# Deferring RMSNorm past the K, V and f projections, with a reordered first stage, in an eight-core attention and gMLP step

## The chip, the cores and the metric

One Trainium2 chip, all eight cores, one launch. Two programs run: even cores (role 0) own 20 of the 32 token blocks of a stream, odd cores (role 1) own the other 12, 32 rows of running streams, and compute K and V of role 0's 20 blocks too, because their attention needs them. The metric is the device time of the slowest core in microseconds. It stands above the spans that the profile lists: by 3.4 to 4.0 us where an even core has the longest span, by 1.0 to 1.1 where an odd one is longest by 3 us or more. Some executions fall into a slower state, in which the cores of one die show a lower granted clock and take longer (in one run of the twelfth kernel 0.816 to 0.830 and 1753 to 1800 us on die 0, against 0.987 to 0.995 and 1520 to 1529 us on die 1); only fast runs are compared.

## The reference, cut to what matters

```python
def rmsnorm(x, g):
    y = x * lax.rsqrt(jnp.mean(x * x, axis=-1, keepdims=True) + RMS_EPS)
    return y * g
def mixer_layer(x, norm_g, w_in, b_f, ln_g, ln_b, w_s, b_s, w_out, caches=None):
    h = rmsnorm(x, norm_g)
    z = h @ w_in                 # columns [q | k | v | f | g_A | u | v_B | g_B], D = 2048
    logf = log_sigmoid(f + b_f)
    v_b  = layernorm(gelu(v_B), ln_g, ln_b)
    out_a = fox_attention(q, k, v, logf) * silu(g_A)      # 8 heads of 128, causal
    out_b = gelu(u) * (tril(w_s) @ v_b + b_s) * silu(g_B) # chunks of 128 positions
    y = x + concat(out_a, out_b) @ w_out                  # a last rmsnorm follows
    return y, k, v, logf, v_b                             # k, v, logf are outputs too
```

With r = 1/sqrt(mean(x²)+eps), one number per token, h @ W = r · ((x·g) @ W). The norm can therefore be applied after a projection as well as before it.

Of the kernel before, what the change touches and what calls it, by code (L numbers as in the profile page):

```python
# [12 lines left out]
D = 2048  # L13
KC = 16
# [106 lines left out]
class Arena:  # L121
# [18 lines left out]
    def alloc(self, name, shape, dt, nres=1, hi=False):  # L140
        n = int(np.prod(shape)) * (4 if dt in (F32, I32) else 2)
        n = (n + 63) // 64 * 64
        gaps = self.gaps(n)
        assert gaps, ("arena full", name, n, [(t.name, t.hi - t.lo) for t in self.live])
        lo = gaps[-1][1] - n if hi else gaps[0][0]
        t = Tile(name, lo, lo + n, shape, dt, self.ap, nres)
        for d in self.dead:
            if d.lo < t.hi and t.lo < d.hi:
                for r in t.res:
                    for o in d.res:  # L150
                        r.inherit(o)
        self.live.append(t)
        self.peak = max(self.peak, max(x.hi for x in self.live))
        return t
# [51 lines left out]
def build_program(only_role=None):  # L206
# [8 lines left out]
    def dscr(name, shape, dt=BF16):  # L215
# [17 lines left out]
        KT_s=dscr("KT_s", [8, 128, NBLK * 128]), V_s=dscr("V_s", [8, 128, NBLK, 129]),  # L233
# [25 lines left out]
def emit(ctx, role):  # L259
# [28 lines left out]
    def load(q, out, in_, res, part=False, reads=()):  # L288
        q.dma(out, in_, dsem_of(res), reads=reads, writes=[] if part else [res], pwrites=[res] if part else [])
# [24 lines left out]
    if smp:  # L314
# [3 lines left out]
    POOL.op(lambda: g.memset(ones[:], 1.0), writes=[ones.r])  # L318
    POOL.op(lambda: g.memset(utri[:], 1.0), writes=[utri.r])
    POOL.op(lambda: g.affine_select(out=utri[:], in_=utri[:], pattern=[[1, 128]], compare_op=ALU.is_ge,  # L320
                                    fill=0.0, base=0, channel_multiplier=-1), reads=[utri.r], writes=[utri.r])
    POOL.op(lambda: g.tensor_scalar(out=utrih[:], in0=utri[:], scalar1=0.5, scalar2=None, op0=ALU.mult), reads=[utri.r], writes=[utrih.r])
# [3 lines left out]
    H = HTok(A, [(t * 512, 512) for t in range(NT)] if role == 0 else [(0, 768), (768, 800)])  # L326
    WK = [A.alloc("WK%d" % h, [KC, 128], BF16) for h in range(8)]
    VW = [384, 384, 264]
    WV = [A.alloc("WV%d" % c, [KC, VW[c]], BF16) for c in range(2 if role == 0 else 3)]
    hTb, Vf, Vb = [], [], []  # L330
    v_ready = False
    xt = [A.alloc("xt%d" % i, [2, KC, 128], F32, nres=2, hi=(i == 2)) for i in range(3)]
    sq = [A.alloc("sq%d" % i, [KC, 64], F32) for i in range(2)]
    ssp = A.alloc("ssp", [256], F32)
    rb = [A.alloc("rb%d" % i, [256], F32) for i in range(2)]
    NKS = 3
    Kb = [A.alloc("Kb%d" % i, [512], BF16) for i in range(NKS)]
    if role:
        Vb = [A.alloc("Vb%d" % i, [8, 129], BF16) for i in range(2)]
    Kf = [A.alloc("Kf%d" % i, [512], F32, hi=True) for i in range(NKS)]  # L340
    R_KTs, R_Vs = Res("KT_s"), Res("V_s")

    xq = []
    if role == 0:
        groups = [("own", list(range(4 * i, 4 * i + 4))) for i in range(NT)]
        passes = [("K", i) for i in range(NT)] + [("V", i) for i in range(NT)]
    else:
        groups = [("own", list(range(4 * i, 4 * i + 4))) for i in range(NT)] + [("smp", [0])]
        groups += [("oth", list(range(4 * i, 4 * i + 4))) for i in range(o0 // 4)]
        passes = [("K", i) for i in range(NT + 1)] + [("V", i) for i in range(NT + 1)]  # L350
        for i in range(NT + 1, len(groups)):
            passes += [("K", i), ("V", i)]
        passes[-3:-1] = [passes[-2], passes[-3]]
    def ng_of(n):
        return 0 if n < 2 else 8

    nunits, pairs = [], []
    for gi, (kind, bl) in enumerate(groups):
        for p0 in range(0, len(bl), 2):
            pr = dict(kind=kind, bl=bl[p0:p0 + 2], tile=None)  # L360
            nunits.append(dict(gi=gi, pr=pr, ii=[p0 + i for i in range(len(pr["bl"]))], kind=kind, bl=pr["bl"]))
            pairs.append(pr)
    xfree = {"tiles": [0, 1, 2], "next": 0}

    def x_next():
        while xfree["next"] < len(pairs):
            pr = pairs[xfree["next"]]
            ok = [t for t in xfree["tiles"] if t < 2 or pr["kind"] != "oth"]
            if not ok:
                return  # L370
            t = pr["tile"] = ok[0]
            xfree["tiles"].remove(t)
            xfree["next"] += 1
            for a, j in enumerate(pr["bl"]):
                if pr["kind"] == "smp":
                    load(SP, xt[t][:, a, :, 0:NS2], io["xsT"], xt[t].res[a])
                else:
                    load(SP, xt[t][:, a, :, :], io["xT"][(o0 if pr["kind"] == "own" else 0) + j], xt[t].res[a])

    def ninfo(n):  # L380
        u = nunits[n]
        rows = NS2 if u["kind"] == "smp" else 128
        na = len(u["ii"])
        t = xt[u["pr"]["tile"]]
        return u, na, rows, na * rows, t[:, 0:na, :, 0:rows], t.res[0:na]

    def norm_a(n):
        u, na, rows, w, x, rx = ninfo(n)
        step = min(rows, 64)
        for c in range(w // step):  # L390
            t = sq[c % 2]
            a, n0 = c * step // rows, c * step % rows
            ACT.op(lambda: act.activation(out=t[:, :, 0:step], in_=x[:, a, :, n0:n0 + step], func=AF.Square), reads=rx, writes=[t.r])  # L393
            DVE.op(lambda: v.tensor_reduce(out=ssp[:, c * step:(c + 1) * step], in_=t[:, :, 0:step].rearrange("p k n -> p n k"),  # L394
                                           axis=AX.X, op=ALU.add),
                   reads=[t.r], writes=[ssp.r] if c == 0 else [], pwrites=[] if c == 0 else [ssp.r])
        for k in range(ng_of(n)):
            ACT.op(lambda: act.activation(out=x[:, :, k, :], in_=x[:, :, k, :], func=AF.Copy, scale=gcol[:, k:k + 1]),  # L398
                   reads=rx + [gcol.r], writes=rx if k == 0 else [], pwrites=[] if k == 0 else rx)

    def norm_b(n):
        u, na, rows, w, x, rx = ninfo(n)
        r = rb[n % 2]
        mmop(PSB[7][:, 0:w], ones[:, :], ssp[:, 0:w], True, True, [ones.r, ssp.r], 7, True, True)
        ACT.op(lambda: act.activation(out=r[:, 0:w], in_=PSB[7][:, 0:w], func=AF.Ln, scale=1.0 / D, bias=RMS_EPS),
               reads=[PSR[7]], writes=[r.r])
        ACT.op(lambda: act.activation(out=r[:, 0:w], in_=r[:, 0:w], func=AF.Exp, scale=-0.5), reads=[r.r], writes=[r.r])  # L407
        if u["kind"] == "own":
            c0 = u["bl"][0] * 128
            dst, rd = H.at(c0, w), H.res(c0, w)  # L410
        elif u["kind"] == "smp":
            dst, rd = H.at(TO, w), H.res(TO, w)
        else:
            t = hTb[(u["gi"] - NT - 1) % 2]
            dst, rd = t[:, :, u["ii"][0] * 128:u["ii"][0] * 128 + w], [t.res[i] for i in u["ii"]]
        NG = ng_of(n)
        for a in range(na if NG else 0):
            DVE.op(lambda: v.tensor_tensor(out=dst[:, 0:NG, a * rows:(a + 1) * rows], in0=x[:, a, 0:NG, :],  # L418
                                           in1=r[:, a * rows:(a + 1) * rows].unsqueeze(1).broadcast_to([128, NG, rows]), op=ALU.mult),
                   reads=rx + [r.r], writes=[rd[a]])  # L420
        for k in range(NG, KC):
            DVE.op(lambda: v.scalar_tensor_tensor(out=dst[:, k, :].rearrange("p (a n) -> p a n", a=na), in0=x[:, :, k, :],  # L422
                                                  scalar=gcol[:, k:k + 1], in1=r[:, 0:w].rearrange("p (a n) -> p a n", a=na),
                                                  op0=ALU.mult, op1=ALU.mult),
                   reads=rx + [gcol.r, r.r], writes=rd if k == 0 else [], pwrites=[] if k == 0 else rd)
        xfree["tiles"].append(u["pr"]["tile"])
        xfree["tiles"].sort()

    order = []
    for n in range(len(nunits)):  # L430
        order += [("a", n), ("b", n)]
    order_pos = {s: i for i, s in enumerate(order)}
    state = {"pos": 0, "k": 0}

    def norm_to(pos):
        while state["pos"] < min(pos, len(order)):
# [137 lines left out]
    for c in range(len(WV)):  # L574
        wv_load(c)
# [820 lines left out]
```

## The kernel before: the parts that the change and the argument touch

A core works through five stages: (1) norm, K, V and f; (2) v_B with GELU and LayerNorm; (3) u, g_B and the chunk mixing; (4) attention, with the q and g_A projections of the next head as filler between its matmuls; (5) the output projection. x comes transposed, features on partitions, in blocks of 128 tokens; a pair of blocks is one unit of work. PE is TensorE, DVE VectorE, ACT ScalarE, POOL GpSimd, SP the engine that issues most stores.

The norm of a pair stands in front of its first matmul:

```python
def norm_a(n):                                    # squares and their sum
    for c in range(w // step):                    # step = 64 tokens
        ACT.op(... activation(out=sq, in_=x[...], func=AF.Square))
        DVE.op(... tensor_reduce(out=ssp[...], in_=sq, axis=AX.X, op=ALU.add))
    ...
def norm_b(n):
    mmop(PSB[7][:, 0:w], ones, ssp[:, 0:w], ...)  # sum over partitions, broadcast
    ACT.op(... activation(out=r, in_=PSB[7], func=AF.Ln, scale=1.0 / D, bias=RMS_EPS))
    ACT.op(... activation(out=r, in_=r, func=AF.Exp, scale=-0.5))
    ...                                           # h = x * g * r, on DVE
    DVE.op(... scalar_tensor_tensor(out=dst[:, k, :], in0=x[:, :, k, :], scalar=gcol[:, k], in1=r, ...))
```

K leaves PSUM through ACT into one of three staging tiles; POOL makes a bf16 copy, and SP stores both:

```python
ACT.op(... activation(out=Kf[s], in_=PSB[bank], func=AF.Copy), writes=[Kf[s].r])
POOL.op(... tensor_copy(out=Kb[s], in_=Kf[s]))
store(SP, io["kT"][...], Kf[s]);  store(SP, io["KT_s"][...], Kb[s])   # output, bf16 scratch
```

Role 0 makes K of all its pairs, then V of all: `passes = [("K", i) ...] + [("V", i) ...]`.

## Time and profile before

The kernel before took 1601.92 us (median of five runs, one of them slow; later 1601.0 of fifteen, two of them slow). Its stages, read from the start of the last V eviction, the last tanh of stage three, the first and the last exp of attention, in us:

| | stage 1 ends | stages 2 and 3 | to first exp | attention's exps | rest | span |
|---|---|---|---|---|---|---|
| core 0 (role 0) | 387.8 | 423.5 | 40.4 | 447.4 | 288.9 | 1588.0 |
| core 7 (role 1) | 591.9 | 279.6 | 26.1 | 505.9 | 195.1 | 1598.6 |

The prediction below reads the rows by stage. The 315 to 331 that it gives for core 7 are GB/s, and its L791 is an addition of two fp32 tiles of 128x1024 on DVE. "Cold clock" is its estimate of the time lost where the granted clock is below 1.00, as on core 7 from 120 to 140 and from 715 to 735 us, at 0.83. One cut that it does not make is needed later: stage one of core 0, divided where PE has done its first 80 us of work and at its last longer wait. In these rows the columns are start:end and length, busy time and instruction count of PE, PEld, DVE, ACT and POOL, the granted clock, the busy share of the DMA engines, and GB/s.

```profile
0.00:128.00 128.00, 80.01 (x652) 66.91 (x652) 78.92 (x97) 57.52 (x89) 19.26 (x42) 0.97 0.79 221
128.00:281.00 153.00, 118.43 (x892) 92.19 (x893) 53.37 (x62) 49.81 (x88) 22.24 (x33) 0.88 0.74 154
```

PE idles 48 us in the first piece and 34.6 us in the second, and the second runs at a mean clock of 0.88. So the idle time is not only a matter of the start: it goes on for 280 us. In the second piece PE waits for h, and ACT for staging tiles that K stores hold (total us, times, longest):

```profile
PE psb L301 <- DVE arena L422: 35.9, 5, 14.8
...
ACT arena L495 <- DMA kT<-arena: 23.3, 6, 7.7
```

### The profile page before, as it was taken

What the parts mean: (1) busy time and instruction counts of PE and PEld (TensorE: products, weight loads), DVE (VectorE), ACT (ScalarE), POOL (GpSimd) and SP (SyncE); (2) the same over time, 40 slices, a digit from 0 to 9 for tenths busy, and PEclk for the clock granted to TensorE, in tenths of its full rate; (3) what the DMA queues carried; (4) which work ended last, traced back from release to release, by engine and by line L of the source; (5) the groups of instructions that cost most, each with busy time, mean ns of one, the idle gap of its engine ahead of it and who ended that gap; (6) DMA issues with size and microseconds to landing.
All of it is one profiled execution on the core that took longest, in us unless ns stands there. A gap on an engine that the chain in (4) does not pass through costs nothing.

```text
span 1598.6 us, 32756 instructions; the slowest of 8 cores (1580.1 to 1598.6 us)
## 1 busy us (share of the span) xinstructions
PE 1462.1 (91%) x12204; PEld 981.5 (61%) x12204; DVE 507.7 (32%) x922; ACT 776.8 (49%) x1345; POOL 159.6 (10%) x266
## 2 busy tenths in 40 slices
PE   0896889798989899998999999999999999999997
PEld 0675557575858654455666677777777776644443
DVE  3861720533524013444335111212111112123333
ACT  2452622433433016631111688898898988921112
POOL 1012111000000102321000211101101111100000
PEclk9998999999999999999999999999999999999999
DMA  6949764534321930005323937447256154835653
GB/s 190 273 146 167 218 154 90 132 81 92 92 82 38 181 51 21 1 30 140 67 57 81 165 51 147 104 71 137 73 76 117 34 111 104 175 118 161 202 153 99
DMA packets 140612, 179.15 MB, mean 112 GB/s; under 512 B 80576, under 2 KB 118720, under 8 KB 130560
## 3 DMA queue, kind: packets, MB, share of 16 engines
q1 hardware_dynamic: 93824, 122.41, 26.6%
q0 software_dynamic: 46624, 54.56, 21.7%
q8 instruction: 102, 1.67, 0.4%
q14 instruction: 62, 0.51, 0.1%
HBM read 182.37 MB, written 49.14 MB: 145 GB/s over the span
## 4 chain that ended last, share of the span: by engine, by line
PE 72%; DVE 9%; ACT 7%; DMA 5%; issue 4%; POOL 1%; SPq 1%; ACTq 0%; DVEq 0%; POOLq 0%
PE psb L301 72%; DVE arena L394 3%; DVE arena L422 3%; ACT arena L398 2%; DMA kT<-arena 2%; ACT arena L1083 2%; DMA V_s<-arena 2%; DVE arena L418 1%; ACT arena L393 1%; DMA arena<-xT 1%; DMA KT_s<-arena 0%; POOL arena L789 0%; SPq L115 0%; PE psb L1156 0%; DVE arena L1094 0%
## 5 line engine op out<-in xcount | busy, mean ns | idle before, releaser
L301 PE MATMUL psb<-arena 128*128 128x129 bf16 (+11 forms) x12100 | 1459.8, 280 | 128.0 <-DVE arena L394 37.4
L301 PEld LDWEIGHTS psb<-arena 128*128 128x128 bf16 (+2 forms) x12100 | 976.3, 99 | 606.8 <-issue 183.8
L1083 ACT ACTIVATE arena<-psb,arena 128x512 bf16<-128x512 f32 (+3 forms) x672 | 433.0, 664 | 47.0 <-PE psb L301 28.2
L394 DVE TENSOR_REDUCE arena<-arena 128x64 f32<-128x1024 f32 (+1 forms) x65 | 119.1, 1894 | 16.6 <-ACT arena L393 16.6
L393 ACT ACTIVATE arena<-arena 128x1024 f32<-128x1024 f32 (+1 forms) x65 | 66.4, 1044 | 98.0 <-DVE arena L394 97.9
L1298 ACT ACTIVATE arena<-arena 128x2048 bf16<-128x2048 f32 x12 | 22.9, 1910 | 145.4 <-DVE arena L1293 145.4
L533 ACT ACTIVATE arena<-psb 128x384 bf16<-128x384 f32 (+1 forms) x40 | 16.3, 441 | 117.5 <-PE psb L301 98.3
L418 DVE TENSOR_TENSOR arena<-arena 128x1024 bf16<-128x1024 f32 (+1 forms) x29 | 34.7, 1234 | 119.4 <-ACT arena L407 119.4
L524 DVE TENSOR_TENSOR arena<-psb,arena 128x8 f32<-128x8 f32 (+1 forms) x33 | 5.2, 163 | 205.0 <-PE psb L301 205.0
L955 DVE SCALAR_TENSOR_TENSOR arena<-arena,psb 128x512 bf16<-128x512 f32 (+1 forms) x32 | 18.7, 585 | 154.6 <-ACT arena L954 95.5
L398 ACT ACTIVATE arena<-arena 128x256 f32<-128x256 f32 (+1 forms) x120 | 59.5, 496 | 11.4 <-ACT arena L398 0.4
L1086 POOL TENSOR_SCALAR_AFFINE_SELECT arena<-arena 128x128 bf16<-128x128 bf16 x96 | 27.9, 292 | 344.5 <-ACT arena L1083 342.8
L422 DVE SCALAR_TENSOR_TENSOR arena<-arena 128x256 bf16<-128x256 f32 (+1 forms) x152 | 60.4, 471 | 4.4 <-ACT arena L407 4.4
L864 ACT ACTIVATE arena<-psb 128x384 f32<-128x384 f32 (+1 forms) x32 | 15.9, 498 | 85.8 <-PE psb L301 65.8
L935 DVE CAST arena<-psb 128x400 bf16<-128x400 f32 (+1 forms) x28 | 15.8, 565 | 127.6 <-PE psb L301 127.6
L1293 DVE TENSOR_TENSOR arena<-psb,arena 128x512 f32<-128x512 f32 x48 | 29.8, 683 | 66.6 <-PE psb L301 66.3
L492 ACT ACTIVATE arena<-psb 128x512 bf16<-128x512 f32 x40 | 22.5, 592 | 54.1 <-PE psb L301 47.6
L859 ACT ACTIVATE arena<-psb 128x384 bf16<-128x384 f32 (+1 forms) x32 | 15.8, 497 | 61.1 <-PE psb L301 61.0
L789 POOL TENSOR_TENSOR arena<-arena 128x1024 f32<-128x1024 f32 (+1 forms) x13 | 30.5, 2345 | 134.8 <-DVE arena L787 134.8
L888 DVE TENSOR_TENSOR arena<-psb,arena 128x512 f32<-128x512 f32 (+1 forms) x32 | 17.9, 561 | 66.9 <-PE psb L301 66.9
L539 ACT ACTIVATE arena<-psb 128x384 f32<-128x384 f32 (+3 forms) x39 | 14.6, 457 | 48.4 <-PE psb L301 48.4
L1142 DVE SCALAR_TENSOR_TENSOR arena<-psb,arena 128x128 bf16<-128x128 f32 x96 | 33.7, 351 | 11.0 <-DVE arena L1142 0.5
(101 smaller groups left out, 431.4 us busy)
## 6 DMA issues: line engine op xcount, KB each, us to landing
arena<-xT SPq DMA_DIRECT2D x32, 1024.0 KB, 8.6
arena<-xn SPq DMA_DIRECT2D x12, 1024.0 KB, 8.9
y<-arena SPq DMA_DIRECT2D x12, 1024.0 KB, 6.0
V_s<-arena SPq DMA_DIRECT2D x32, 258.0 KB, 6.0
arena<-V_s SPq DMA_DIRECT2D x8, 1032.0 KB, 8.6
KT_s<-arena SPq DMA_DIRECT2D x64, 128.0 KB, 2.8
arena<-KT_s SPq DMA_DIRECT2D x8, 1024.0 KB, 5.0
arena<-ckT POOLq DMA_DIRECT2D x16, 512.0 KB, 10.7
```

Source lines behind the costliest of these rows:

```text
L301: PE.op(lambda: mm(out, lhsT, rhs, start=start, stop=stop, **kw), reads=reads, writes=[PSR[bank]] if first else [], pwrites=[] if first el ...
L393: ACT.op(lambda: act.activation(out=t[:, :, 0:step], in_=x[:, a, :, n0:n0 + step], func=AF.Square), reads=rx, writes=[t.r])
L394: DVE.op(lambda: v.tensor_reduce(out=ssp[:, c * step:(c + 1) * step], in_=t[:, :, 0:step].rearrange("p k n -> p n k"), axis=AX.X, op=ALU.add),
L398: ACT.op(lambda: act.activation(out=x[:, :, k, :], in_=x[:, :, k, :], func=AF.Copy, scale=gcol[:, k:k + 1]), reads=rx + [gcol.r], writes=r ...
L418: DVE.op(lambda: v.tensor_tensor(out=dst[:, 0:NG, a * rows:(a + 1) * rows], in0=x[:, a, 0:NG, :], in1=r[:, a * rows:(a + 1) * rows].unsque ...
L422: DVE.op(lambda: v.scalar_tensor_tensor(out=dst[:, k, :].rearrange("p (a n) -> p a n", a=na), in0=x[:, :, k, :], scalar=gcol[:, k:k + 1], ...
L789: POOL.op(lambda: g.tensor_tensor(out=vt[q, :], in0=vt[q, :], in1=lngb[q, :], op=ALU.mult), reads=[vt.r, lngb.r], writes=[vt.r])
L1083: ACT.op(lambda: act.activation(out=P[:, off:512], in_=PSB[b][:, off:512], func=AF.Exp, scale=SCALE, bias=nb[:, T, j, h:h + 1]), reads=[PS ...
L1086: POOL.op(lambda: g.affine_select(out=P[:, off:off + 128], in_=P[:, off:off + 128], pattern=[[1, 128]], compare_op=ALU.is_ge, fill=0.0, ba ...
L1142: DVE.op(lambda c=c, q=q, ps=ps: v.scalar_tensor_tensor(out=o[:, 2 * c + q, :], in0=ps[:, q, 0:128], scalar=rc[:, 2 * c + q:2 * c + q + 1] ...
L1293: DVE.op(lambda cg=cg, b=b: v.tensor_tensor(out=yb[p][q, cg * 512:(cg + 1) * 512], in0=PSB[b][q, :], in1=xr[p][q, cg * 512:(cg + 1) * 512] ...
L1298: ACT.op(lambda: act.activation(out=junk[q, :], in_=yb[p][q, :], func=AF.Square, accum_out=ss), reads=[yb[p].r], writes=[junk.r, R_ss[p]])
```

## The change

Its intent: PE multiplies bf16(x·g), which needs no sum of squares, and r is applied when K, V and f leave PSUM; h itself, which later stages use, is scaled afterwards and only for own blocks. Around that, much else moves. Cut to its core:

```diff
+    def g_mul(n):            # x*g to bf16: k < 10 on DVE, the rest on ACT
+        DVE.op(... tensor_scalar(out=o, in0=x[:, :, k, :], scalar1=gcol[:, k:k + 1], op0=ALU.mult))
+        ACT.op(... activation(out=o, in_=x[:, :, k, :], func=AF.Copy, scale=gcol[:, k:k + 1]))
+    def square(n):           # ACT squares x in place, POOL adds the halves
+    def tree(n):             # DVE adds the rest;  rms(n): ones-matmul, Ln, Exp
-            ACT.op(... activation(out=Kf[s], in_=PSB[bank], func=AF.Copy))
-            POOL.op(... tensor_copy(out=Kb[s], in_=Kf[s]))
+        DVE.op(... tensor_tensor(out=ov, in0=PSB[bank], in1=rb.broadcast, op=ALU.mult))   # K: r as a row
+            ACT.op(... activation(out=o, in_=src, func=AF.Copy, scale=rc))                # V: r per token
+    def h_scale(n, k):       # own h times r, afterwards, on DVE
-    NKS = 3
+    Kf = [A.alloc("Kf%d" % i, [512], F32, hi=True) for i in range(6)]   # 2 after the ramp
-            store(SP, io["KT_s"]..., Kb[s])          # own blocks
+        load(POOL, KTh[p][...], io["kT"][...])       # attention reads own K, V from the fp32 outputs
-    passes = [("K", i) for i in range(NT)] + [("V", i) for i in range(NT)]
+    ramp = [("G", 0), ("S", 0), ("K", 0, 0), ("G", 1), ("T", 0), ...]   # K of five pairs
+    # then V of these five, then K and V pair by pair; norms sorted in by time
+                    load(POOL, WVB[c]...)            # v_B weights 2 and 1 pairs before the end
-    vt = A.alloc("vt", [1024], F32)
+    vtb = A.alloc("vt", [1024], F32) if smp else None    # role 0: LayerNorm in place in gx
+    lead = qga(0)                                    # head 0's q and gate only as far as needed,
+    while (0, "g", torder[0]) not in done: next(lead)    # the rest as filler in attention
```

The first part, K of the first five pairs while x and the weights are still coming in, is called the ramp. Line numbers in rows of the changed kernel: L385 and L387 scale x by g, L394 squares, L395, L402 and L403 add, L450 evicts K, L490 V, L568 is the late scaling of h.

> **What bounds the kernel now.** Even cores (role 0: 20 of 32 token blocks, no streams) and odd cores (role 1: 12 own blocks, 32 stream rows, and K and V of the 20 other blocks) run different programs, so I read both. First the cores' spans: 1580.1 to 1588.0 us on even cores, 1596.9 to 1598.6 on odd ones, granted clocks alike (a fast state); the odd ones end last by 11 us. Then busy time by stage, cut at the last K/V eviction, the start of u/g, of attention and of the output projection:
>
> ```profile
> core 0: us, PE busy (x) PEld busy (x) DVE busy (x) ACT busy (x) POOL busy (x), PEclk, DMA share, GB/s
> 0.00:388.00 388.00, 304.50 (x2260) 229.59 (x2260) 134.80 (x173) 125.52 (x225) 58.23 (x91) 0.94 0.70 167
> 388.00:525.00 137.00, 136.94 (x636) 62.44 (x637) 51.65 (x144) 77.45 (x192) 45.24 (x23) 1.00 0.22 30
> 525.00:824.00 299.00, 297.70 (x1546) 141.57 (x1544) 116.75 (x194) 55.02 (x95) 18.65 (x21) 1.00 0.27 54
> 824.00:1315.00 491.00, 483.81 (x5487) 355.62 (x5488) 135.13 (x355) 324.30 (x523) 62.13 (x188) 1.00 0.33 76
> ...
> core 7: us, PE busy (x) PEld busy (x) DVE busy (x) ACT busy (x) POOL busy (x), PEclk, DMA share, GB/s
> 0.00:592.00 592.00, 487.36 (x3794) 370.37 (x3794) 226.69 (x300) 202.21 (x364) 43.97 (x75) 0.95 0.55 133
> 592.00:694.00 102.00, 98.69 (x467) 46.13 (x468) 37.47 (x107) 57.09 (x139) 28.64 (x13) 1.00 0.07 16
> 694.00:897.00 203.00, 196.12 (x1366) 121.21 (x1364) 82.70 (x169) 35.90 (x72) 17.68 (x23) 0.98 0.38 88
> ```
>
> From the second stage on PE is busy over 96% of the time at full clock. The first stage (norm, K, V) is different: 84 us of idle PE on core 0, 105 us on core 7, and a clock of 0.94 and 0.95. No other engine is full there (DVE 135 of 388). So latency, not throughput, costs the time. The view of waits names it, for PE in the first 400 us of core 0 and 600 us of core 7:
>
> ```profile
> PE psb L301 <- DVE arena L422: 52.6, 10, 14.8
> PE psb L301 <- DVE arena L394: 26.1, 5, 20.8
> ...
> PE psb L301 <- DVE arena L394: 37.4, 7, 30.4
> PE psb L301 <- DVE arena L422: 30.7, 4, 11.8
> PE psb L301 <- ACT arena L492: 22.6, 3, 8.3
> PE psb L301 <- ACT arena L533: 7.0, 2, 6.4
> ```
>
> L394 is the sum of squares, L422 the multiplication that writes h: PE waits for a normalised h. The chain of core 0 shows what holds that chain up in its turn:
>
> ```profile
> 128.38 9.33 SPq L115
> 137.76 1.50 SPq L115
> 139.36 13.33 DMA kT<-arena
> 152.81 0.45 issue
> 154.25 0.90 DVE arena L418
> ```
>
> A K store, issued behind loads on a blocked SP queue, holds a staging tile; the K eviction on ACT waits for it, the next block's r = exp(-0.5 ln) stands behind that eviction on ACT, h behind r, and PE behind h.
>
> [...] with x and K weights both queued, the DMA share is 1.0 from 20 to 80 us. [...] core 7, loading x alone at 13 to 26 us, moved 315 to 331. [...] 20 us slices of core 7 with a long gap show 0.83, the second stage 1.00, so removing gaps returns more than the gaps. [...] L791 took 1.225.
>
> **The change, part by part.**
> (1) The norm leaves PE's path: PE multiplies bf16(x*g) and r enters at the evictions: K on DVE (row r), V and f by a per-token scale on ACT/DVE. h itself is scaled afterwards, own blocks only. Squares are summed by ACT, a POOL halving and a DVE tree. A pair of blocks now costs DVE 10 scalings (estimate 0.3 us each, from 0.81 for 1024 at L787) = 3.0, tree 1.2+0.7+0.4 = 2.3, four K evictions at 0.69 = 2.8, f 0.3, late h scaling 4 x 1.23 = 4.9: 13.3 us. ACT: 6 scalings of 0.5, 2 squares of 2 (L1298 takes 1.91), V 6 x 0.46, logs 1.2: 11 us. POOL: 2 x 2.35. All below PE's 28 us, so hidden.
> (2) PE's floor. K: 185 matmuls of 256 columns in the slice 500 to 520 = 108 ns, 128 a pair = 13.8 us. V: core 7's last four blocks came 7.00 us apart, 14.0 a pair. The fp32 ones-matmul 0.64 us, with two new one-column ones (estimate) 0.95. Pair: 28.8. Role 0: 10 pairs = 288 us. Role 1: 16 pairs = 460, stream rows 3.5+7+1: 472. Before, the same sum (without the 0.3) is 284 and 467, against 388 and 592.
> (3) Start. One half block of x suffices instead of two blocks, squares, sum, Ln/Exp and scaling; x no longer delays the K weights. First K matmuls before: 29.7 (core 0) and 39.4 us (core 7); x landed at 10.9 and 20.5. With about 2 us of scaling: 13 and 20.
> (4) The ramp becomes DMA-bound. K of five pairs needs x 5 x 2.1 = 10.5 MB and weights of 8.4 MB (fp32 as read), in the order they are consumed; with K stores of 5.2 MB and the first V weights of 6.3 this is 30 MB, 92 us at 330 GB/s. PE's part is 5 x 14.8 = 74 us after the start. Stepping through (2 weights and one pair of x = 4.2 MB = 13 us each step, PE getting 1, 3, 5, 7 half-bank units from it) gives some 10 to 14 us of waits, and I add 4 for cold clock: the ramp ends near 102 us on both roles.
> (5) After that: V of five pairs 70, then role 0 five pairs 144: 316, plus 2 for stalls: 318. Role 1: 11 pairs 317, stream rows 11, 70: 500, plus 7 for stalls of a longer stage: 507. Gain: 70 us on role 0, 85 on role 1.
> (6) v_B weights are loaded two and one pairs before the end, into freed x tiles. Before, they blocked a V store for 26 us (534 to 560 on core 7); this is inside (5).
> (7) Own K/V scratch stores vanish; attention loads own K/V from the fp32 outputs by GpSimd DMA with a cast: twice the bytes and, for V, 512-byte pieces (2560 a head on role 0). A head takes 61 us, the comparable cvn load 13 us to landing: hidden.
> (8) Mixing is delayed by 7 tiles for the first group. Before, core 7's PE waited 1.7+3.8 us for W_s (721 and 726), with some 2 of cold clock: -7 on role 1; nothing on role 0.
> (9) Most of head 0's q and gate moves into attention (27 us on role 0, 15 on role 1). Attention is already full of PE work, so it is moved, not saved; only the idle 2.1+1.4 us at core 0's entry can go: -2.
> (10) On role 0 LayerNorm now works in place in gx. Chain from the odd gelu (471.16) to the end of its last add: 14.05 us, against PE's 13.8 a pair. 0.3 us a pair over 9 pairs is below the 5 us that the PSUM banks buffer: 0.
> Sum, role 0: 1588-70-2 = 1516. Role 1: 1598.6-85-7-2 = 1505. The slow role changes; the kernel ends with role 0. The runs' median is 2 us above the profiled one and the ramp may do a little better: **1515 us**, 0.946 of before.
>
> **Rivals.**
> (A) DMA takes the place of the norm: K stores queue behind the V weights in the ramp again, DVE stops at a full staging tile and with it the scaling of the next x. For: 30 MB in 100 us, and the 13 us store above. Against: six staging tiles instead of three, no KT_s stores for own blocks (a third of the K store bytes), V weights in three steps. Worth 10 to 25 us: 1525 to 1540.
> (B) Attention pays: GpSimd carries K/V loads, weights and the diagonal masks in one order, or ACT (449 of 527 us on core 7) cannot feed more PE work. For: ACT is at 85%. Against: PE is at 98% there already and its total work is unchanged; the K/V load is issued when its buffer has just come free. 5 to 30 us: 1520 to 1545.
> (C) The ramp hardly waits, because x and weights arrive interleaved, and role 0 reaches its floor: first stage 288+13+4 = 305: 1500; moved fillers covering attention's 7 us of idle on role 0 give 1493.
> (D) The first stage is hidden anyway: it would need another bound; no engine is full there and everything later waits for it in PE order. I give this 1%.
>
> **Range and chances.** The floor of 288 and 472 us is measured rate times count; the uncertain terms are ramp waits (+-8), steady stalls (+-5), attention (-5 to +20). That makes 1492 to 1538. The 2% line is 1570: it would take losing 55 of 70 us. Faster 0.95, within 2% 0.04, slower 0.01.
>
> **What would show it.** First stage ending near 318 (core 0) and 507 us (core 7), PE idle there 25 to 35 us, most before 102 us; first K matmul at 13 and 20 us; waits of PE on the squares gone; core 7 without the W_s wait near the first mixing; stages two to five as long as before within 3 us, save that entry to attention moves some 27 us earlier and attention grows by as much on role 0; even cores ending last. Wrong: PE waiting on DVE whose release is a kT store (A); longer attention in total (B); a first stage on role 1 above 525, which would make odd cores last again.

## The result, and the profile after

1529.89 us (median of eight runs, 1527.5 to 1532.3) against 1601.02 (median of fifteen, two of them slow). The ratio is 0.956, with a 95% interval of 0.955 to 0.957. Ratios are the mean time of one kernel's fast runs over that of the other's fast runs in the same rounds, so not quite the ratio of the medians quoted. The prediction of 1515 was 15 us too low, within its range. As predicted the slow role changed: even cores span 1524.6 to 1526.0 us, odd ones 1513.5 to 1517.8.

| | stage 1 ends | stages 2 and 3 | to first exp | attention's exps | rest | span |
|---|---|---|---|---|---|---|
| core 0 | 326.8 | 426.7 | 9.6 | 473.9 | 287.9 | 1524.9 |
| change | −61.0 | +3.2 | −30.8 | +26.5 | −1.0 | −63.1 |
| core 7 | 519.2 | 279.7 | 11.8 | 511.3 | 195.3 | 1517.3 |
| change | −72.7 | +0.1 | −14.3 | +5.4 | +0.2 | −81.3 |

The gain is stage one on both roles. Rows by stage of the changed kernel; the first four are core 0, the others core 7:

```profile
0.00:108.00 108.00, 79.49 (x703) 70.45 (x704) 36.62 (x92) 36.90 (x59) 34.12 (x36) 0.95 0.92 234
108.00:327.00 219.00, 215.77 (x1631) 160.69 (x1632) 76.64 (x136) 65.08 (x118) 27.70 (x18) 0.99 0.50 143
...
327.00:485.00 158.00, 156.64 (x720) 70.05 (x721) 73.04 (x175) 82.56 (x204) 47.01 (x20) 1.00 0.04 11
...
763.00:1254.00 491.00, 485.69 (x5498) 356.66 (x5499) 137.97 (x359) 321.60 (x520) 73.15 (x200) 1.00 0.42 75
...
0.00:519.00 519.00, 478.70 (x3893) 376.04 (x3893) 164.47 (x358) 164.42 (x292) 95.64 (x72) 0.99 0.51 139
...
799.00:811.00 12.00, 10.90 (x116) 7.71 (x113) 7.78 (x14) 3.60 (x6) 9.97 (x15) 1.00 1.07 164
811.00:1343.00 532.00, 517.70 (x5981) 377.18 (x5982) 97.43 (x270) 450.42 (x727) 72.58 (x160) 1.00 0.63 107
```

PE has its first 79.5 us of work done at 108 us instead of 128, so the ramp gained 20 us. After it PE idles 3.2 of 219 us; before, the same rest took 260 us, of which PE idled 35.5. So 41 of the 61 us were gained after the ramp: 32 us of idle time, and 9 us of busy time, which is 215.8 us at a clock of 0.99 where it was 224.5 at 0.92. On core 7, the slow one before, the ramp ends at 121 us where PE had done as much at 128, so it gained only 7; the rest took 398 us in place of 464. The experiments come back to this split. In stage one of core 0, 83.5 us of idle PE (388 − 304.5) became 31.7. What is left, in the view of PE's waits (total us, times, longest):

```profile
PE psb L301 <- DMA arena<-wk: 17.8, 3, 12.9
PE psb L301 <- DVE arena L385: 9.8, 1, 9.8
...
PE psb L301 <- DVE arena L450: 2.2, 1, 2.2
```

The sum of squares is gone from the list but for 0.9 us. The first matmul waits 12.9 us for x and the first K weights, the second pair of x costs 9.8 us. The chain of core 0 (start, length, what) shows what these waits stand for:

```profile
3.75 13.35 DMA arena<-wk
...
17.55 17.35 DMA arena<-xT
...
37.97 21.17 PE psb L301 x172
...
62.39 23.80 DMA kT<-arena
```

Two loads, and a K store of 256 KB that took 23.8 us beside x, V weights and other K stores; it cost PE only 0.9 us, as the staging tiles took most of it. The second pair of x (2.1 MB) took 17.35 us, some 121 GB/s, while the K weights were in the other queue. The two queues shared the DMA engines, in unequal parts: from 17.5 to 34.9 us the queue with x moved 320 of 799 packets and took 40% of the engines' time, the casting queue 478 and 62%.

On core 7 the wait for W_s near the first mixing went, as step (8) said, and another came:

```profile
637.38 0.34 SPq L115 DMA_DIRECT2D arena<-bs  x1
...
651.02 0.55 POOL L115 DMA_DIRECT2D arena<-wu  x1
...
664.33 25.96 PE L301 MATMUL psb<-arena 128*128 128x384 bf16 x153 [6.27 <-DMA arena<-wu]
```

POOL waits for the mixing bias, prepares the mixing constants, and only then issues the next u weights; PE waits 6.3 us for them. They are not the only thing that ends then: DVE, stopped in the mixing by a store of its output (oT_s), comes free within 0.1 us of the weights' landing, and on cores 3 and 5 the same wait of 5.4 to 5.7 us is put down to DVE.

### The profile page after: what moved, and what is told of

It is laid out like the page before. It is cut to its first block, busy times and chain, and to the rows that moved or that the text cites. A ratio compares the mean times of both kernels' runs of the same rounds, so it can differ in the third digit from the quotient of the medians.

```text
span 1526.0 us, 30007 instructions; the slowest of 8 cores (1513.5 to 1526.0 us)
## 1 busy us (share of the span) xinstructions
PE 1476.6 (97%) x11216; PEld 908.7 (60%) x11216; DVE 539.1 (35%) x1062; ACT 603.6 (40%) x1051; POOL 199.1 (13%) x298
## 4 chain that ended last, share of the span: by engine, by line
PE 85%; DMA 5%; DVE 3%; issue 3%; POOL 2%; ACT 2%; POOLq 0%; DVEq 0%; SPq 0%; ACTq 0%
PE psb L301 84%; DMA kT<-arena 3%; POOL arena L792 2%; DMA arena<-xT 1%; DVE arena L568 1%; DMA arena<-wk 1%; DVE arena L790 1%; PE psb L1177 1%; ACT arena L763 0%; DMA arena<-lng 0%; ACT psb L768 0%; ACT arena L1104 0%; DVE arena L385 0%; DVE arena L794 0%; DVE arena L1163 0%
## 5 line engine op out<-in xcount | busy, mean ns | idle before, releaser
L301 PE MATMUL psb<-arena 128*128 128x512 bf16 (+5 forms) x11056 | 1473.4, 296 | 39.5 <-DMA arena<-wk 16.2
L301 PEld LDWEIGHTS psb<-arena 128*128 128x128 bf16 x11056 | 901.2, 99 | 606.2 <-issue 50.7
L1104 ACT ACTIVATE arena<-psb,arena 128x512 bf16<-128x512 f32 x480 | 303.0, 633 | 151.3 <-PE psb L301 146.1
L1322 ACT ACTIVATE arena<-arena 128x2048 bf16<-128x2048 f32 x19 | 36.3, 1910 | 224.5 <-DVE arena L1317 224.5
L1317 DVE TENSOR_TENSOR arena<-psb,arena 128x512 f32<-128x512 f32 x76 | 47.2, 683 | 110.1 <-PE psb L301 110.1
L976 DVE SCALAR_TENSOR_TENSOR arena<-arena,psb 128x512 bf16<-128x512 f32 x40 | 27.5, 687 | 149.8 <-ACT arena L975 91.1
L490 ACT ACTIVATE arena<-psb,arena 128x384 f32<-128x384 f32 (+1 forms) x60 | 30.4, 543 | 125.5 <-PE psb L301 109.9
L395 POOL TENSOR_TENSOR arena<-arena 128x1024 f32<-128x1024 f32 x20 | 46.9, 2366 | 198.4 <-ACT arena L394 198.4
L792 POOL TENSOR_TENSOR arena<-arena 128x1024 f32<-128x1024 f32 x20 | 47.0, 2348 | 135.9 <-DVE arena L790 89.1
L890 DVE SCALAR_TENSOR_TENSOR arena<-arena,psb 128x512 bf16<-128x512 f32 x40 | 27.5, 688 | 103.9 <-ACT arena L889 101.8
L450 DVE TENSOR_TENSOR arena<-psb,arena 128x512 f32<-128x512 f32 x40 | 26.7, 689 | 90.2 <-PE psb L301 34.2
L394 ACT ACTIVATE arena<-arena 128x2048 f32<-128x2048 f32 x20 | 37.1, 1901 | 38.0 <-DVE arena L385 38.0
L568 DVE TENSOR_TENSOR arena<-arena 128x1024 bf16<-128x1024 bf16 x40 | 48.7, 1265 | 0.0
L1325 DVE SCALAR_TENSOR_TENSOR arena<-arena 128x2048 f32<-128x2048 f32 x19 | 44.7, 2351 | 2.4 <-DVE arena L1324 0.6
L910 DVE TENSOR_TENSOR arena<-psb,arena 128x512 f32<-128x512 f32 x40 | 27.6, 691 | 46.1 <-PE psb L301 46.1
L385 DVE TENSOR_SCALAR arena<-arena 128x256 bf16<-128x256 f32 (+1 forms) x110 | 28.5, 337 | 31.5 <-DMA arena<-xT 31.5
```

The costliest lines, as they stand in the source:

```text
L301: PE.op(lambda: mm(out, lhsT, rhs, start=start, stop=stop, **kw), reads=reads, writes=[PSR[bank]] if first else [], pwrites=[] if first el ...
L394: ACT.op(lambda: act.activation(out=x, in_=x, func=AF.Square), reads=[t.res[a]], writes=[t.res[a]])
L395: POOL.op(lambda: g.tensor_tensor(out=x[:, 0:8, :], in0=x[:, 0:8, :], in1=x[:, 8:16, :], op=ALU.add), reads=[t.res[a]], writes=[t.res[a]])
L490: ACT.op(lambda: act.activation(out=o, in_=src, func=AF.Copy, scale=rc), reads=[PSR[bk[c]], rr], writes=[dst.r] if first else [], pwrites= ...
L568: DVE.op(lambda: v.tensor_tensor(out=hv[:, k:k + 4, :], in0=hv[:, k:k + 4, :], in1=rb.unsqueeze(1).broadcast_to([128, 4, units_n[n]["w"]]) ...
L792: POOL.op(lambda: g.tensor_tensor(out=vt[q, :], in0=vt[q, :], in1=lngb[q, :], op=ALU.mult), reads=[vt.r, lngb.r], writes=[vt.r])
```

## The experiments

Twelve runs on three chips. The kernel before took 1607 us on the first two and 1601 on the third; the changed kernel, which was run again on the second, took 1531.4 there (ratio 0.953) and 1529.9 at first (0.956). So the first eight are compared with 0.953 and 1531.4, the last four with 0.956. Times are medians of fast runs (the third, fourth and seventh kernel had one slow run each, the ninth three, the twelfth two). "Stage one" is the start of the last V eviction of core 0 and of core 7.

| | time, us | ratio to before | stage one, cores 0 / 7 |
|---|---|---|---|
| 5 changed kernel again | 1531.4 | 0.9531 ± 0.0019 | 326.9 / 518.4 |
| 1 norm back, no look-ahead | 1596.3 | 0.9927 ± 0.0025 | 394.9 / 593.2 |
| 2 v_B weights late | 1533.0 | 0.9530 ± 0.0023 | 323.9 / 521.5 |
| 3 head 0's q and gate first | 1534.2 | 0.9539 ± 0.0030 | 327.5 / 518.7 |
| 4 x before weights | 1532.6 | 0.9528 ± 0.0029 | 329.4 / 520.3 |
| 6 norm back, look-ahead | 1558.0 | 0.9699 ± 0.0019 | 356.1 / 549.5 |
| 7 V weights later | 1527.6 | 0.9512 ± 0.0023 | 324.7 / 514.6 |
| 8 scratch stores back | 1539.5 | 0.9584 ± 0.0019 | 336.7 / 522.6 |
| 9 norm, ACT, stores back | 1573.0 | 0.9828 ± 0.0020 | 371.0 / 559.8 |
| 10 three staging tiles | 1542.2 | 0.9633 ± 0.0016 | 335.6 / 526.4 |
| 11 LayerNorm edits | 1528.7 | 0.9551 ± 0.0015 | 327.4 / 520.9 |
| 12 all that looked good | 1529.9 | 0.9555 ± 0.0013 | 325.4 / 517.8 |

All outputs were correct. Theory 1 is the prediction's: the gain is the latency of the norm in front of PE. The first rival is that the reordered loads, the larger staging and the dropped stores gave it, and the deferral is incidental.

**The control.**

> The changed kernel itself, unedited, as the control for the runs beside it, since chips differ: the first four experiments ran on a chip whose kernel before took 1607 us. Ratio to before 0.956 within 0.003; first V eviction of core 0 at 111 us and last one at 327 us, within 2 us.

Ratio 0.9531, first V eviction at 110.7, last at 326.9: as expected.

**Norm back, twice.** First with every pair's norm in order before its K units:

```diff
-    ramp = [("G", 0), ("S", 0), ("K", 0, 0), ("G", 1), ("T", 0), ...]
+    for n in range(5): ramp += [("G", n), ("S", n), ("T", n), ("R", n)] + K units of step n
         elif what == "R":
             rms(n)
+            for k in range(0, KC, 4): h_scale(n, k)      # before the K matmuls
-   K: in1=rb      V, f: scale=rcol      late h_scale
+   K: in1=ones    V, f: scale=ones      none
-    [(24, "G"), (19, "S"), (9.5, "T"), (4, "R")]         # lead of each step after the ramp, us
+    [(32, "G"), (27, "S"), (17.5, "T"), (12, "R")]
```

> The changed kernel with the norm put back into PE's path: each pair of blocks is scaled by r (the same four late-scaling operations on DVE) before its first K matmul, and the evictions keep their form but multiply by one. Loads, staging tiles and the dropped scratch stores stay as in the changed kernel. Theory 1 (the gain is the latency of the norm in the first stage): the first K matmul of an even core moves from 13 to about 28 us, every pair of the ramp comes some 10 us later, the first stage grows by 30 to 50 us, time 1555 to 1580. Rival (the gain is the order of the loads, six staging tiles and fewer stores, and the deferral is incidental): first stage longer by less than 12 us, time below 1542.

It lost 65 us, more than theory 1 gave it: all in the ramp, where each pair's scaling stood on DVE behind the K evictions of the pair before, so that PE waited some 13.3 us for it four times over. That is a fault of the edit's order. The second try emits scaling, squares and tree of the next pair ahead of this pair's K units, and its ones-matmul before the last of them.

> As the first experiment (norm in PE's path), but with a fair order: scaling, squares and tree of the next pair are emitted ahead of the K units of this pair, and its ones-matmul before the last of them, so that each pair's norm can run while PE multiplies the pair before. The first experiment had no such look-ahead and lost 72 us in the ramp alone. Theory 1 (the latency of the norm itself, from the landing of x to the scaled h, costs the time wherever PE has no other work): the first pair still starts at 32 instead of 13 us and the second pair comes 11 us later; first V eviction of core 0 at 135 to 155 us instead of 111, time 25 to 45 us above the control. Rival (the first experiment lost its time only by its poor order): within 12 us of the control.

26.6 us above the control, stage one 29 us longer, first V eviction at 144.2: theory 1. PE on core 0, start, length, what, and in brackets the idle time before it and its releaser (L403 is the end of the tree, L423 the scaling of h):

```profile
24.49 1.84 PE L301 MATMUL psb<-arena 128*128 128x256 f32 x6 [24.49 <-DVE arena L403]
32.30 5.36 PE L301 MATMUL psb<-arena 128*128 128x128 bf16 x64 [5.97 <-DVE arena L423]
46.96 7.37 PE L301 MATMUL psb<-arena 128*128 128x256 f32 x38 [9.30 <-DVE arena L403]
...
87.71 252.52 PE L301 MATMUL psb<-arena 128*128 128x256 f32 x1985 [6.19 <-DVE arena L403]
```

The first K matmul moves from 13 to 32 us, and there are waits up to 88 us. But then PE does not stop any more, though every pair is normalised before its matmuls. With the new order the norm in PE's path costs 27 us: the first V eviction comes 33.5 us later, and what follows is 6 to 7 us shorter, as the late scalings are gone. The idle time that the kernel before had from 128 to 281 us needs another cause.

**Scratch stores back.** The dropped stores for own K and V, with the same bytes and piece sizes, to a tensor that nobody reads:

```diff
             store(SP, io["kT"]..., ov, dst.r, R_kT)
+            store(SP, io["KT_x"]..., ov[:, :, 0:w // 2], dst.r)    # half the fp32 columns
                 store(SP, io["vo"]..., o, dst.r, R_vo)
+                store(SP, io["V_x"]..., first 64 of each 128 columns of o, dst.r)
```

> Each own K and V store is followed by a second store of half its fp32 columns into a scratch tensor nobody reads: the same bytes and piece sizes as the bf16 scratch stores that the change dropped (512 bytes for K, 256 for V). Theory 1 (step 7 and rival A: DMA bounds the ramp, so these bytes would come back as waits on K stores): 2.1 MB more in the ramp at some 310 GB/s are 7 us, and the staging tiles are held twice as long: first stage 5 to 12 us longer, time 4 to 12 us above the control. Rival (stores are hidden behind six staging tiles): within 2 us of the control.

8.1 us above the control and stage one 9.8 us longer: theory 1. PE's waits for K evictions grew from 2.5 to 10.2 us, half of it in the ramp and half at the end of the stage. The DMA engines were busy for 94.4% of the first 110 us in the control and for 96.5% here, and the stores that were called hidden were not.

**Three staging tiles.** `range(6)` to `range(3)` for the K staging tiles in the ramp.

> The changed kernel with three instead of six K staging tiles in the ramp; the deferred norm stays. Theory 1 (the deferred norm frees PE from the stores: DVE stops in evictions, but no r is needed for the next K matmuls; only the scaling of the next x is behind them): PE waits on DVE grow by 3 to 10 us in the ramp, time 3 to 10 us above the control's 1531. Rival (six tiles are what gave the gain): 20 us or more above it.

The ratio is 0.0073 above 0.956, 11.7 us: just outside theory 1's 3 to 10, far from the rival's 20. DVE sat at a full set of tiles, and PE behind it:

```profile
72.90 0.69 DVE L450 TENSOR_TENSOR arena<-psb,arena 128x512 f32<-128x512 f32 x1 [19.71 <-DMA kT<-arena]
...
73.74 12.17 PE L301 MATMUL psb<-arena 128*128 128x256 bf16 x96 [9.57 <-DVE arena L450]
```

So rival A of the prediction, a K store that stops the evictions, is real; the six tiles are what kept it to 2 us.

**Norm, ACT evictions, three tiles and stores back together.** This asks whether the rest of the gain is the coupling that the prediction quotes: a K store holds a tile, ACT stops in an eviction, the next norm stands behind it.

```diff
 (as "norm back, look-ahead" and "scratch stores back", and)
-        DVE.op(... tensor_tensor(out=ov, in0=PSB[bank], in1=ones, op=ALU.mult))
+        ACT.op(... activation(out=ov, in_=PSB[bank], func=AF.Copy))
-    Kf = [... for i in range(6)]     # 2 after the ramp
+    Kf = [... for i in range(3)]     # 3 after the ramp
```

> The sixth experiment (norm back in PE's path with look-ahead, 26.6 us above the control) with, in addition, what the kernel before had around it: K evictions on ACT, three K staging tiles, and the scratch stores of the eighth experiment (8.1 us alone). Theory 1, extended (the missing third of the gain is the coupling: K stores hold three staging tiles, ACT stops in an eviction, and Ln and Exp of the next norm stand behind it, as the chain quoted in the prediction shows): more than the sum of 26.6 and 8.1, time 1580 to 1605, with PE waiting for the scaled h whose release is a K store in the chain. Rival (no coupling, the parts add): 1562 to 1570, and the rest of the gain lies in something not tried.

Its fast runs took 1572 to 1574 us (three more were slow). The two parts by themselves came to 0.0168 and 0.0053 of ratio, together 0.9781; this run has 0.9828, 7 to 8 us more, and 1573 lies between the two forecasts. But that sum leaves out the three tiles, 0.0073 by themselves in the run above. With them the parts add to 0.9854, more than was measured, so a cost of the coupling beyond its parts is not shown. The coupling itself is in the chain of core 0 as described, a store, the scaling on ACT behind it, then the squares and the sum, then PE:

```profile
48.14 33.36 DMA KT_x<-arena
...
82.08 2.50 ACT arena L387 x6
...
84.66 1.92 ACT arena L394
...
94.33 14.04 PE psb L301 x102
```

But again it acts in the ramp alone. Rows of stage one, cut where PE has been busy for 79.6 us (at a clock of 0.86 that is 628 matmuls, where the changed kernel had done 703):

```profile
0.00:148.00 148.00, 79.61 (x628) 68.50 (x629) 52.27 (x106) 46.86 (x79) 33.70 (x36) 0.86 0.78 200
148.00:371.00 223.00, 222.13 (x1707) 167.51 (x1704) 49.57 (x95) 76.60 (x138) 27.68 (x18) 1.00 0.61 167
```

After the cut PE idles 0.9 us, on core 7 after its ramp 0.5 us, with the norm in its path, ACT evictions, three tiles and all stores. The kernel before idled 34.6 us there at a clock of 0.88. So none of these gave the 41 us. What this run still has of the new kernel is the order (V of five pairs follows the ramp, then K and V of a pair in turn), with norms issued ahead by time, and the new form of squares and sums. Before, role 0 made K alone of the fifth to tenth pair before any V, so that a norm was wanted for every 13.8 us of PE work; now it is one for every 28. The old norm could not keep up with 13.8: on core 0 the logarithms (L405 there) of four pairs in a row came 20.1, 19.6 and 24.3 us apart.

```profile
153.27 0.39 ACT arena L405
...
173.41 0.38 ACT arena L405
...
192.96 0.39 ACT arena L405
...
217.22 0.39 ACT arena L405
```

Between them ACT waited for DVE's sums of the squares, with the K evictions behind. One norm for 28 us of work would fit such a pace, so the order would be enough; a shorter norm might be enough too. On core 7, whose other blocks had K and V in turn before as well, 22.6 of the 57 us that PE idled after 128 us were waits for K evictions (L492), and these stood behind the next squares on ACT, which speaks for the new form there. No run changed the order or the form alone: how the 41 us divide between them stays open.

**Loads of the ramp, twice.** After its first matmul, PE's longest wait is for the second pair of x. First attempt:

```diff
-    load(SP, x pair 1, 2, reads=[WK[2 * n - 1].r])      # each waits for a K weight
+    load(SP, x pair 1, 2)                               # issued at once
-    K weights 2 to 7, then V weights 0, issued together
+    K weights 2, 3; then 4, 5 behind the squares of pair 0, 6, 7 of pair 1, V weights 0 of pair 2
```

> In the ramp the second and third pair of x are issued at once, behind the first, and K weights 4 to 7 and the first V weights only behind the squares of pairs 0, 1 and 2, so that x does not share the DMA engines with weights that are needed later. Theory 1 (PE's 11.7 us wait for the second pair is x sharing the engines with weights not yet needed): the second pair lands near 28 instead of 35 us on even cores, that wait falls to 3 to 6 us, first stage and time shorter by 4 to 8 us: 1522 to 1526. Rival (the DMA engines are full throughout, so order does not matter): later waits grow by the same amount, time within 2 us of 1530.

The rival was right, 1.2 us slower than the control and within the intervals. The second pair landed at 31.4 instead of 35 us and its wait went (the 1.7 us below is for the third pair), but others took its place:

```profile
PE psb L301 <- DMA arena<-wk: 22.4, 5, 13.4
PE psb L301 <- DVE arena L450: 7.7, 3, 4.4
...
PE psb L301 <- DVE arena L385: 1.7, 1, 1.7
```

The second attempt keeps the place of x, and moves K weights 6 and 7 and all V weights one step later.

> K weights 6 and 7 are issued behind the squares of pair 1, the first V weights behind those of pair 2, the second at the end of the ramp, the third inside the V units; x keeps its places. Theory 1, after the experiment with x first (the ramp is bound by DMA until about 47 us, and order alone moves waits around): fewer bytes ahead of the second and third x pair do help, because 3.1 MB of V weights and 2.1 MB of K weights leave the first 47 us; PE's waits in the ramp after the first matmul fall from 15 to 5 to 9 us; time 5 to 9 us below the control. Rival (the waits only move again, to the K stores and the V weights): within 2 us of the control.

3.8 us below the control, but the intervals overlap. The wait for the second pair stayed (12.2 us), so theory 1 of that run fell; stage one of core 0 ended 2.2 us earlier. An estimate says why little is to be had. Up to the first K units of the third pair PE needs three pairs of x (6.3 MB) and six K weights (6.3 MB as fp32). The ramp of the changed kernel moved 17.5 MB of plain traffic and 7.7 MB of casting loads, 15.5 MB as read, in some 104 us: 317 GB/s. At that rate the 12.6 MB take 40 us from the first load at 3.75, so until about 44 us, and by then PE has six units of 3.7 us to do: some 22 us of idle time that no order of these loads removes as long as PE takes its units in this order. It had 27.6.

**The v_B weights late.** The load goes back behind the last K units.

> The v_B weights are loaded as before, behind the last K units, into the freed K weights, instead of one and two pairs earlier into freed x tiles. Theory 1 (step 6): 8.4 MB of fp32 behind the last K stores take some 25 to 30 us, of which PE covers the last 14 us of V, so stage one or the first block of the next stage waits 10 to 20 us longer: even cores 1536 to 1546. Rival (the weights arrive in time anyway, the early load only moves the queueing): within 3 us of the changed kernel, 1527 to 1533.

Time 1.6 us above the control, within the intervals and on the upper edge of the rival's band, but neither story is quite right. Stage one of core 0 ended 3.0 us earlier, as the weights now come behind the last K stores (in the changed kernel the last weights were issued at 291.8 us, and a K store issued at 298.5 took 18.0 us), then PE waited 5.0 us for the weights on core 0 and 7.7 on core 7, whose mean granted clock was 0.986, against 0.993 in the control. Odd cores lost more: core 7 needed 288.9 us from there to its last tanh instead of 279.5. The early load is worth some 2 us of time at most.

**Head 0's q and gate first.** `for _ in lead: pass` in place of stopping at the first need.

> All of head 0's q and gate before attention, as before the change. Theory 1 (step 9: the work is moved, not saved): last g tanh to first exp longer by some 25 to 31 us on even cores, the exps shorter by about as much; even cores longer by 2 to 6 us in all, time 1530 to 1536. Rival (attention has spare PE time that the filler uses): time longer by 15 to 27 us.

On even cores as theory 1 says: entry longer by 28 us, exps shorter by 26, time 2.8 us above the control, within the intervals. On odd cores not: entry +14.3 on core 7, exps only −3.0, so it lost 11 us (the other three lost 8 to 10), and the odd cores ended as late as the even ones. Rows of core 7 in this run, entry and attention:

```profile
800.00:826.00 26.00, 24.14 (x287) 18.69 (x284) 10.54 (x19) 4.80 (x8) 2.58 (x5) 1.00 0.38 83
...
826.00:1355.00 529.00, 515.41 (x5811) 369.41 (x5812) 95.06 (x265) 448.79 (x725) 79.97 (x171) 1.00 0.63 107
```

With the same 6,098 matmuls (6,097 in the rows of the changed kernel above, from 799 to 1343), PE counts as busy for 539.6 us here and for 528.6 us there, at 15.4 us of idle time in both. So on odd cores a busy PE in attention had some 11 us of room, which the busy share of 98% hid.

**The LayerNorm stage.** Three edits at once, for the 3.2 us that the stage grew by on role 0:

```diff
-    vtb = A.alloc("vt", [1024], F32) if smp else None
+    vtb = A.alloc("vt", [1024], F32)                  # apart from gx again
-    A.free(*(ssp + [lnt]))
+    A.free(*(ssp + [lnt, rbw]))                       # in the room of the r rows
+    load(SP, lngb ...); load(SP, lnbb ...)            # right behind the ring, not behind the lf store
-            for _ in range(len(arg[1]) // 2 + 1):     # late scalings per V unit
+            for _ in range(len(arg[1]) // 2 + 2):
```

> The LayerNorm stage on even cores: a separate output tile again in place of gx (in the room of the r rows, which are dead by then), the two LayerNorm vectors loaded right behind the ring instead of behind the log-gate store, and one more late scaling per V unit so that fewer than the 14 of now remain at the end. Theory 1 (the stage grew by 3 us because of the in-place tile and the late start of its loads): last V eviction to last g tanh of core 0 back from 427.8 to 423.5 to 425 us, time 2 to 4 us below 1531. Rival (late scalings cost DVE time before the end of V instead): V units and the end of stage one longer by as much, time within 1 us.

From the last V eviction to the last tanh core 0 took 424.0 us, 3.8 less than the control: theory 1 for the stage. For the time the rival: the ratio is 0.9551 against 0.956, 1.4 us and within the intervals. The earlier late scalings slowed V on odd cores (first to last V eviction 401.9 and 398.8 us on cores 1 and 7, 395.3 and 395.2 in the control), and one odd core had the longest span (1527.2 us; the even cores reached 1525.0). Which of the three edits did what is open, but in the first experiment, with no late scalings at all and LayerNorm in place, the same stretch took 425.6 us, so some 1 to 2 us (426.7 and 427.8 in the two profiles of the changed kernel) are the 14 late scalings that stood on DVE before LayerNorm.

**All that looked good.** The V weights later, the LayerNorm edits, a third staging tile after the ramp, and head 0's K/V load behind the first u and g weights of the ring (`kv_load(0)` moved from before the u/g loop to behind its first g chunk), so that core 7 need not wait for u weights.

> Together: weights later (seventh experiment, -3.2 us), the LayerNorm edits of the eleventh, a third K staging tile after the ramp against the 2.5 us wait on a K store at the end of stage one, and head 0's K/V load behind the second pair of u/g weights, so that odd cores do not wait 6 us for them. If the parts add: 3.2 + 3 + 2 = 8 us below 1531, 1521 to 1525, with odd cores 6 us shorter too. If the waits only move: 1526 to 1529.

No better: 0.9555. Even cores ended at 1520.9 to 1524.3, but odd ones, at 1524.4 to 1527.3, now ended last. The u weights came in time on core 7, and a longer wait took their place:

```profile
652.98 46.66 SPq L115 DMA_DIRECT2D oT_s<-arena  x10
...
669.80 0.19 DVE L920 TENSOR_TENSOR arena<-arena 128x32 bf16<-128x32 f32 x1 [10.79 <-DMA oT_s<-arena]
...
673.08 27.14 PE L301 MATMUL psb<-arena 128*128 128x384 bf16 x165 [13.59 <-DVE arena L894]
```

The K/V load and the weights now run together, the small stores of the mixing stand behind them, DVE stops at its store tile, and PE 13.6 us behind DVE. This is the store that had already ended together with the weights in the changed kernel, so taking the weights away could not have been enough. No run beat the changed kernel by more than the intervals.

## Why the prediction was right or wrong, point by point

The direction, the change of the slow role, and the stage that would pay were right. The miss of 15 us against the time comes from several terms. The predicted span of role 0 was 1516, it is 1524.9: 9 us from stage one and 3.2 from LayerNorm, less 2.3 of attention and 1 at the end. The rest is that the time lies 5 us above core 0's span (3.7 above the longest even one, where before it lay 1.1 above the longest odd one); I had allowed 2 and taken them off again for a better ramp.

- (1) The norm leaves PE's path. Right in that PE's waits for squares went, and that the new work of DVE, ACT and POOL is hidden (in stage one of core 0 they were busy for 113, 102 and 62 of 327 us). Wrong in what it explains. I read the whole idle time of stage one as the norm's latency. With the new order, putting the norm back cost 26.6 us, all in the ramp; after the ramp PE idled 0.9 us even with ACT evictions, three tiles and the scratch stores back. The 41 us after the ramp on core 0, and 66 on core 7, came with the new order and the shorter norm, neither of which the prediction treated as a cause; which of them did how much is not shown.
- (2) The floor of 288 us for role 0: PE was busy for 295 us. The excess is mostly clock, by an estimate: at 0.95 the first 79.5 us of busy time hold 4 us of it, at 0.99 the other 215.8 hold 2.
- (3) The start was right on role 0 (12.9 us for 13) and late on role 1 (24.3 for 20).
- (4) The ramp ends at 108 instead of 102 us on role 0: PE waited 15.6 us after its first matmul, where I had 10 to 14, and the lower clock, 0.95 over these 108 us, took by the estimate in (2) the 4 us that I gave it. The 30 MB were too few as well: they count x of five pairs, but the next two pairs were issued within the ramp, which moved 33 MB as read. On role 1 the first V eviction came at 123.9, so the ramp ended near 121. Of these 19 us, 7 are a slip of the sum: "the ramp ends near 102 us on both roles" leaves out that role 1 starts 7 us later by step (3); 4 more are its late start. It is the largest single error of the working, and it cost nothing in the time, as odd cores end early.
- (5) After the ramp role 0 took 219 us for 216 and role 1 398 for 405: the 7 us for stalls did not come.
- (6) The v_B weights: late loading costs 1.6 us of time, within the noise, not the 26 us that the stalled store of the kernel before suggested. What was inside (5) was small.
- (7) Attention's loads from the fp32 outputs are hidden, as said: on core 0 they took a median of 9.1 us for K and 11.7 for V from issue to landing, and no instruction is listed as waiting for them. I gave the dropped stores no value of their own; they are worth 8.1 us.
- (8) The W_s wait went, and nothing was gained on role 1: the ring's weights stand behind the mixing constants on POOL, and DVE behind a store of the mixing. I had not asked what comes next on these engines.
- (9) Moved, not saved: right on role 0, −4.3 us for −2. On role 1 −8.9 us, because a busy PE was not a full one: the two rows of core 7 differ by 11 us of busy time for the same matmuls.
- (10) The 5 us that the PSUM banks buffer were my estimate; in the kernel before, ACT had read a block's two banks 4.4 to 5.8 us before PE was done with the next block (L761, core 0). LayerNorm in place costs no more than some 1 to 2 us, but the 14 late scalings that fell into that stage cost 1 to 2 more. I had counted them as hidden because DVE is half idle on average (busy for 73.0 of 158 us in that stage); at the seam of two stages it was not.

Of the rivals, A (a K store takes the place of the norm) happened in small: 0.9 us in the ramp and 2.2 at the end of stage one; three tiles in place of six would have made it 12 us. B did not come. C named the lower bound well but not the loads; its 305 us give 1503 by the prediction's own sum, not 1500. D was wrong, as expected. The range is not the sum of its terms either: from 1515 they add to 1497 to 1548, not 1492 to 1538. And the DMA share of 1.0 from 20 to 80 us is core 7's; core 0 had 0.82 from 60 on.

The step that failed is the valuation of (1), which gave all of the 70 us to the norm's latency in PE's path where putting it back cost 27, together with the missing step for the order and the shorter norm. That the total came out nearly right is because the floor of (2) was taken from measured rates and the new kernel reaches it whatever the reason: as to the cause, that was luck.

## What to carry to other kernels

When idle time is removed, ask of each stretch whether the latency went or the work beside it grew: with twice as much PE work per norm (and a shorter norm) it was hidden even in PE's path (0.9 us of idle PE after the ramp of the ninth run), while taking it out of the path mattered only where there was no other work yet. In this ramp, at a DMA share of 0.92, putting the dropped bytes back cost 8.1 us, and reordering the loads mostly moved the wait (1.2 us slower and 3.8 us faster, both within the intervals). And judge a filler's worth by running it, not by the busy share of the engine it would fill.

## What the traces show beside the change

- In the ramp, with plain loads, casting loads and stores mixed and the DMA share at 0.92, core 0 moved 317 GB/s, counting casting loads at their fp32 size. The profile counted them at the size that they have after the cast: its rows give 512 KB for a K weight of 1 MB in fp32, so the 234 GB/s shown for that stretch understate the traffic.
- A K store of 256 KB took 23.8 us in the changed kernel and a scratch store of 128 KB 33.4 us in the ninth run, while 16 K stores in the ramp had a median of 12.4 us.
- The same 6,098 matmuls (6,097 recorded in one run) counted as 528.6 or 539.6 us of busy PE, with only their order changed.
- In the profiled run of the changed kernel, a fast one, all four cores of both dies kept a mean granted clock of 0.991 to 0.995 with PE busy for 95 to 97% of the span (cores 7 and 0). A clock of 0.816 to 0.830 appears in a slow run of the twelfth kernel, on die 0, with 0.987 to 0.995 on die 1. The fast and the slow runs of that kernel were made on one chip.
